# Dilated attention on one Trainium2 core: normalising each block's probabilities before their transpose, in place of scaling the finished outputs

## The chip, the core and the metric

The kernel runs on one core of one Trainium2 chip. The metric is the device time of one execution in microseconds (us); less is better. The engines named below are PE (TensorE: matrix products and transposes, writing to the PSUM banks), DVE (VectorE), ACT (ScalarE), POOL (GpSimd) and SP (which issues the DMAs). All of them run side by side and wait for each other through semaphores; each runs its own instructions in the order in which they were compiled.

## The reference, cut to what matters

One decoder layer with 1024 tokens and 1024 channels. Behind a joint input projection stand two mixers: a gated delta rule (4 heads of 128) and the dilated attention that this change touches (8 heads of 64). Its three branches share one softmax in effect, because their numerators and denominators are brought to a common maximum and added before the one division:

```python
    m_all = jnp.maximum(jnp.maximum(ms[0], ms[1]), ms[2])
    wts = [jnp.exp(mi - m_all) for mi in ms]
    num_tot = wts[0][..., None] * nums[0] + wts[1][..., None] * nums[1] + wts[2][..., None] * nums[2]
    den_tot = wts[0] * dens[0] + wts[1] * dens[1] + wts[2] * dens[2]
    out = num_tot / den_tot[..., None]
```

The mixers' outputs go through one output projection with a residual, then RMSNorm, a gated MLP with a short convolution, and a last RMSNorm. A division of every output row of a head by the denominator of its query gives the same value as a division of every probability of that query before the product with the values; this is the freedom that the change uses.

## The kernel before, in words

The program is emitted by several Python generators ("streams") that a small planner, the class `Weave`, interleaves. The planner keeps a clock `pe` of modelled TensorE time and, for every tile, the modelled time at which it is ready. A product advances the clock by the cost given at its call. An operation of another engine is charged by `account` with a fixed part and a part per element (DVE 0.07 + 0.00105 per element, ACT 0.12 + 0.00085, and 0.28 until the result may be used). A stream that needs a tile yields the time until that tile is ready; meanwhile the planner runs the ready stream with the lowest level number. TensorE's order is thereby fixed when the program is emitted (each PE instruction carries an order token); the order on the other engines is set when the program is compiled.

During the attention the streams that matter are `attention` (level 5) and `dense` (level 9). `dense` computes the input projection column by column; a column is 16 "triplets" of three passes (hi x hi, lo x hi, hi x lo), that is 48 matmuls of 128x128 by 128x512; it fills the clock wherever `attention` yields. The order of its columns is fixed (`DENSE`): the attention's own q, k and v of head pairs 1, 2 and 3, then the four gate columns z. `out_proj` (level 8) starts only when `dense` has ended.

Attention handles one pair of heads at a time (`pi`, 0 to 3), in two halves of the sequence (`hh`), each with four blocks of 128 queries (`u`; block number `n` = 4*hh + u). So there are 4 x 8 = 32 blocks and 8 groups of four. For a block:

- `scores` makes, for each head `e` of the pair, one PSUM bank of scores: 128 or 256 columns of near keys, and 128 (`hh` 0) or 256 (`hh` 1) columns of strided keys. The width `wd` is 256 for block 0, 384 for blocks 1 to 3 and 512 for blocks 4 to 7. DVE adds the mask, writes `sm` and accumulates the negated maximum (the profile lists it as CUSTOM_DVE_ANT and a read of the accumulator into `mx`); ACT takes the exponential in place (`sm<-sm,mx`) and accumulates the denominators into the tile `den` (line 853).
- `turn` transposes the probabilities on PE (`ps<-ident,sm`), and copies the near part to `pt` on DVE and the strided part to `pb` on ACT.
- `values` multiplies `pt` by the values (`ps<-pt,vn`) into the group's bank `po`, where the outputs stand transposed (head dimension on the partitions, queries along the free axis).
- After the group's fourth block `merge_classes` adds the strided part (`ps<-pb,vc`), takes the reciprocals of the group's denominators on DVE (`rd`, 128x8) and spreads them over 64 columns each (`rb`, 128x512).
- `normalise` runs two blocks later, from the list `queue`: four PE transposes turn `rb` (`ps<-ident,rb`), ACT copies them back to `rb`, and DVE multiplies `po` by `rb` into `oT` in another order of columns. SP stores `oT` in the scratch `mixer`, except that of the last group, which stays in SBUF.

The blocks are pipelined by `advance`: `scores(n)`, then `values(n-2)` (and the merge if that block was the fourth of its group), then `turn(n-1)`, then any `normalise` that is due. After the last block `advance(None)` runs four times to drain this.

Of the kernel before, what the change touches and what calls it, by code (L numbers as in the profile page):

```python
# [10 lines left out]
OP = mybir.AluOpType  # L11
# [123 lines left out]
def hybrid_layer(tc, I, out):  # L135
# [14 lines left out]
    def tile_(pool, shape, dt, name, tag, bufs):  # L150
        return wv.slot(pool.tile(list(shape), dt, name=name, tag=tag, bufs=bufs), tag, bufs)
# [75 lines left out]
    def next_bank(tag, *tiles, slack=0.0):  # L227

        while max(wv.need(*tiles), wv.slot_free(tag, 2)) + slack > 1e-3:
            yield max(wv.need(*tiles), wv.slot_free(tag, 2)) + slack  # L230
        return bank(tag)
# [581 lines left out]
    def attention():  # L813
        for h in range(H):
            yield from wv.until(("o", h))
        mks = [A("mk", "go") for _ in range(2)]
        sy.dma_start(mks[0], I["mk"][0])
        sy.dma_start(mks[1], I["mk"][1])
        yield from wv.until(("a", 0, 2))
        qkv = att_load(0)  # L820
        cur = qkv[:2] + (yield from att_values(qkv[2]))
        queue = []

        def mask(n):

            i, o, step, w, m = {0: (0, 128, 352, 128, 2), 1: (1, 0, 128, 128, 3), 2: (1, 384, 128, 128, 3),
                                3: (0, 608, 128, 128, 3)}.get(n, (0, 0, 480 - 32 * n, 256, 2))
            t = mks[i]
            return bass.AP(tensor=t.tensor, offset=t.offset + o, ap=[t.ap[0], [step, m], [1, w]]), m

        def scores(it):
            n, q, k, nb = it["n"], it["q"], it["k"], it["nb"]
            pss = [bank("asc") for _ in range(2)]
            yield wv.need(*pss, q, k)
            k0 = max(n - 1, 0) * P
            n1_, n2_ = (n + 1) * P - k0, P * nb
            wd = n1_ + n2_
            for e, er in enumerate(HALVES):
                mm(pss[e][:, :n1_], q[er, n * P:(n + 1) * P], k[er, k0:k0 + n1_], 0.0009 * n1_)
            for c in range(4):  # L840
                o = slice(32 * c, 32 * c + 32)
                for e, er in enumerate(HALVES):
                    mm(pss[e][o, n1_:wd].rearrange("p (n u) -> p n u", u=32), q[er, n * P + 32 * c:n * P + 32 * c + 32],
                       by_block(k)[er, :4 * nb, c, :], 0.00025 * n2_, tile_position=(64 * e, 32 * c))
            sm = A("sm", "dv*", shape=(P, 2, 512))
            mn = tile_(sp, [P, 2], F32, "mx", "mx", 4)
            mv, m = mask(n)
            for e in range(2):
                ve.tensor_tensor_reduce(out=sm[:, e, :wd].rearrange("p (a b) -> p a b", a=m),
                                        in0=pss[e][:, :wd].rearrange("p (a b) -> p a b", a=m), in1=mv, scale=-0.125,  # L850
                                        scalar=-NEG, op0=OP.add, op1=OP.min, accum_out=mn[:, e:e + 1])
            for e in range(2):
                ac.activation(sm[:, e, :wd], sm[:, e, :wd], AF.Exp, bias=mn[:, e:e + 1], scale=-1.0,
                              accum_out=it["den"][:, n, e:e + 1])
            it.update(sm=sm, wd=wd, n1=n1_, k0=k0)

        def turn(it):
            sm, wd, n1_ = it["sm"], it["wd"], it["n1"]
            it["pt"] = []
            for e in range(2):  # L860
                pt = tile_(sp, [P, 256], F32, "pt", "t1", 3)
                it["pt"].append(pt)
                pp = bank("atr")
                yield wv.need(pp, sm)
                for i in range(wd // P):
                    tp(pp[:, i * P:(i + 1) * P], sm[:, e, i * P:(i + 1) * P])
                ve.tensor_copy(pt[:, :n1_], pp[:, :n1_])
                ac.activation(it["pb"][e][:, it["u"]].rearrange("p b t -> p (b t)"), pp[:, n1_:wd], AF.Copy)

        def values(it):  # L870
            u = it["u"]
            yield wv.need(it["po"], *it["pt"])
            for i in range(it["n1"] // P):
                for e, er in enumerate(HALVES):
                    mm(it["po"][er, u * P:(u + 1) * P], v8(it["vn"])[:, it["k0"] // P + i, er],
                       it["pt"][e][:, i * P:(i + 1) * P], 0.12, u == 0 and i == 0, False, skip_group_check=True)

        def merge_classes(g):
            vcv = g["vc"].rearrange("p (c b d) -> p c b d", c=4, b=2)
            po, nb = g["po"], g["nb"]  # L880
            yield wv.need(*g["pb"])
            for c in range(4):
                for b in range(nb):
                    for e in range(2):
                        er = slice(64 * e, 64 * e + 64)
                        mm(po[er].rearrange("p (u t) -> p u t", u=4)[:, :, 32 * c:32 * c + 32],
                           vcv[:, c, b, er], g["pb"][e][:, :, b, 32 * c:32 * c + 32], 0.14,
                           False, c == 3 and b == nb - 1, skip_group_check=True)
            hh = g["hh"]
            rd = tile_(sp, [P, 4, 2], F32, "rd", "rd", 2)  # L890
            ve.reciprocal(rd, g["den"][:, 4 * hh:4 * hh + 4, :])
            rb = tile_(sp, [P, 512], F32, "rb", "t2", 2)
            ve.tensor_copy(rb.rearrange("p (a d) -> p a d", a=8),
                                  rd.rearrange("p u e -> p (u e)")[:, :, None].to_broadcast([P, 8, 64]))
            g["rb"] = rb

        def normalise(g):
            po, rb, hh = g["po"], g["rb"], g["hh"]
            oT = tile_(sp, [P, 512], F32, "oT", "t2", 2)
            pr = yield from next_bank("atr", rb, slack=ASLACK)  # L900
            for u in range(4):
                tp(pr[:, u * P:(u + 1) * P], rb[:, u * P:(u + 1) * P])
            ac.activation(rb, pr, AF.Copy)
            ve.tensor_tensor(
                oT.rearrange("p (n u c) -> p n c u", n=4, c=4),
                po.rearrange("p (n c u) -> p n c u", n=4, c=4),
                rb.rearrange("p (n c u) -> p n c u", n=4, c=4), op=OP.mult)
            if g["pi"] < 3 or hh == 0:
                sy.dma_start(mixer[4 + g["pi"]][:, half(hh)], oT)
            else:  # L910
                last["oT"] = oT
            if hh == 1:
                wv.done.add(("o", 4 + g["pi"]))


        pipe = []

        def advance(it):
            if it is not None:
                yield from scores(it)  # L920
            pipe.insert(0, it)
            if len(pipe) > 2:
                done = pipe.pop()
                if done is not None:
                    yield from values(done)
                    if done["u"] == 3:
                        yield from merge_classes(done["g"])
                        queue.append([1, done["g"]])
            if len(pipe) > 1 and pipe[1] is not None:
                yield from turn(pipe[1])  # L930
            for q in list(queue):
                q[0] -= 1
                if q[0] < 0:
                    yield from normalise(q[1])
                    queue.remove(q)

        for pi in range(4):
            q, k, vn, vc = cur
            den = sp.tile([P, NCH, 2], F32, name="den", tag="den", bufs=2)
            for hh in range(2):  # L940
                nb = 1 + hh
                if hh == 1 and pi < 3:
                    yield from wv.until(("a", pi + 1, 2))
                    qkv = att_load(pi + 1)
                po = bank("ch")
                pb = [A("pb", "qa", shape=(P, 4, nb, P)) for _ in range(2)]
                if pi == 3 and hh == 1:
                    wv.done.add("last group")
                g = dict(po=po, pb=pb, nb=nb, hh=hh, pi=pi, den=den, vc=vc)
                for u in range(4):  # L950
                    yield from advance(dict(n=4 * hh + u, u=u, q=q, k=k, vn=vn, nb=nb, po=po, pb=pb, den=den, g=g))
            if pi < 3:
                cur = qkv[:2] + (yield from att_values(qkv[2]))
        for _ in range(4):
            yield from advance(None)


# [517 lines left out]
```

## Time and profile before

| what | value |
|---|---|
| median of 3 runs | 1268.12 us (1267.27 to 1270.15) |
| the profiled execution, its own time | 1267.09 us |
| span of its trace, first to last instruction | 1263.9 us |
| mean granted TensorE clock | 0.992 |
| attention, first to last `sm` operation | 319 to 490 us, last `oT` at 498.3 us |
| `dense` ends, `out_proj` starts on PE | 521.7 us |
| PE, DVE, ACT, POOL busy over the span | 98%, 74%, 46%, 4% |

The profile page is one execution. Its first part gives the busy time of each engine. A line of the grouped view reads: source line, engine, operation, output tile <- input tiles, shapes, count | busy us, mean ns of one | idle time of the engine just before them and what ended it. Nearly all helpers record at line 131 (DVE and ACT), 176 (products) or 180 (transposes), so groups are told apart by their tiles. `PEld` is the weight load that precedes each product and overlaps the one before. Matmuls are pipelined: a 128x512 product is listed with 389 ns, while in an undisturbed stretch the next one starts 0.2275 us after it.

### The profile page before, as it was taken

The numbers are of one execution on the slowest core, as the hardware profiler recorded it, in microseconds if no ns is written. First come the engines' busy times: TensorE is split into PE (matmuls) and PEld (weight loads), VectorE is DVE, ScalarE is ACT, GpSimd is POOL, SyncE is SP. The second block draws the span as 40 slices with busy tenths as digits, with TensorE's granted clock in tenths as the row PEclk, the third lists the DMA queues.
The fourth block names the chain that finished last, engine by engine and source line by source line (L and its number), as shares of the span: only waits on it lengthen the run. The fifth ranks groups of instructions, "written<-read, shape, count | busy, mean of one in ns | idle before, by whom it ended". The sixth has DMA issues, their size and how long they took to land.

```text
span 1263.9 us, 18352 instructions
## 1 busy us (share of the span) xinstructions
PE 1240.5 (98%) x7102; PEld 1010.7 (80%) x7102; DVE 940.6 (74%) x1450; ACT 587.5 (46%) x1122; POOL 45.3 (4%) x34
## 2 busy tenths in 40 slices
PE   9999999999999999999999999999999999999996
PEld 7878887888677767878888888888888888787886
DVE  7575984573554455576888988988988979899875
ACT  7355534363544253365554444445445444343541
POOL 0012010022000000000000000000000000000000
PEclk9899999999999999999999999999999999999998
DMA  7022243345322411444323123123122198455623
GB/s 232 28 59 76 101 121 98 134 151 201 103 81 93 141 53 41 126 150 150 117 67 100 60 90 100 56 95 101 53 98 100 50 339 311 149 158 191 199 85 134
DMA packets 77766, 151.41 MB, mean 120 GB/s; under 512 B 21744, under 2 KB 28528, under 8 KB 77680
## 3 DMA queue, kind: packets, MB, share of 16 engines
q1 hardware_dynamic: 77680, 150.25, 36.1%
q8 instruction: 55, 0.90, 0.3%
q14 instruction: 31, 0.25, 0.1%
HBM read 112.21 MB, written 35.91 MB: 117 GB/s over the span
## 4 chain that ended last, share of the span: by engine, by line
PE 81%; DVE 8%; DMA 5%; issue 3%; ACT 2%; SPq 0%; POOL 0%; POOLq 0%; DVEq 0%; ACTq 0%
PE ps L176 42%; PE pa L176 18%; PE pc L176 9%; PE dw L176 8%; PE ps L180 4%; DMA wd<-in_wd 2%; DVE pr L131 2%; DMA r<-upark 1%; DVE x1h L131 1%; DVE kT L131 1%; DVE wd L131 1%; DVE r L131 0%; DMA wst<-in_wu 0%; DVE xr L131 0%; DMA xt<-in_xT 0%
## 5 line engine op out<-in xcount | busy, mean ns | idle before, releaser
L176 PE MATMUL dw<-pr 128*128 128x512 f32 (+1 forms) x984 | 213.4, 377 | 2.8 <-DVE x1h L131 2.0
L176 PEld LDWEIGHTS dw<-pr 128*128 128x128 f32 x984 | 176.1, 188 | 39.1 <-DVE x1h L131 4.2
L176 PE MATMUL ps<-xhi,whi 128*128 128x512 f32 x448 | 187.5, 419 | 2.0 <-DVE xr L131 2.0
L176 PE MATMUL ps<-xhi,wlo 128*128 128x512 f32 x448 | 177.0, 395 | 0.2 <-DVE wlo L131 0.2
L176 PE MATMUL ps<-xlo,whi 128*128 128x512 f32 x448 | 176.4, 394 | 0.0
L176 PE MATMUL pa<-T,pair 128*128 128x512 f32 x528 | 128.6, 393 | 0.7 <-ACT u L131 0.7
L176 PEld LDWEIGHTS pa<-T,pair 128*128 128x128 f32 x528 | 99.8, 189 | 21.8 <-ACT u L131 1.0
L176 PEld LDWEIGHTS ps<-xhi,whi 128*128 128x128 f32 x448 | 85.5, 191 | 19.4 <-issue 3.1
L176 PEld LDWEIGHTS ps<-xhi,wlo 128*128 128x128 f32 x448 | 85.0, 190 | 19.4 <-DVE wlo L131 0.6
L176 PEld LDWEIGHTS ps<-xlo,whi 128*128 128x128 f32 x448 | 85.7, 191 | 13.9
L131 ACT ACTIVATE u<-pa 128x512 f32<-128x512 f32 x44 | 26.3, 599 | 110.6 <-PE pa L176 110.6
L131 DVE SCALAR_TENSOR_TENSOR y<-xu,fcw,y 128x1023 f32<-128x1023 f32 (+1 forms) x44 | 56.4, 1281 | 25.7 <-ACT y L131 25.6
L131 ACT ACTIVATE whi<-wst 128x1024 fp32r<-128x1024 f32 (+2 forms) x38 | 38.6, 1016 | 68.8 <-PE ps L176 58.3
L176 PE MATMUL pa<-B,A 128*128 128x512 f32 x264 | 63.4, 389 | 0.0
L176 PE MATMUL pc<-T,S 128*128 128x512 f32 x264 | 63.4, 389 | 0.0
L176 PE MATMUL pa<-T,S 128*128 128x512 f32 x264 | 63.4, 389 | 0.0
L176 PE MATMUL pc<-B,pair 128*128 128x512 f32 x264 | 63.4, 389 | 0.0
L131 ACT ACTIVATE sm<-sm,mx 128x512 f32<-128x512 f32 (+2 forms) x64 | 41.5, 649 | 42.4 <-DVE mx L131 42.4
L131 DVE TENSOR_TENSOR wst<-wst 128x512 f32<-128x512 f32 x88 | 60.4, 686 | 0.8
L176 PE MATMUL ps<-B,pair 128*128 128x512 f32 x252 | 60.5, 389 | 0.0
L176 PEld LDWEIGHTS pc<-B,pair 128*128 128x128 f32 x264 | 49.6, 188 | 10.3
L176 PEld LDWEIGHTS pa<-B,A 128*128 128x128 f32 x264 | 49.6, 188 | 10.3
(233 smaller groups left out, 2280.4 us busy)
## 6 DMA issues: line engine op xcount, KB each, us to landing
wst<-in_wu SPq DMA_DIRECT2D x44, 512.0 KB, 3.6
wd<-in_wd SPq DMA_DIRECT2D x44, 512.0 KB, 4.0
wst<-in_wi SPq DMA_DIRECT2D x25, 512.0 KB, 3.7
upark<-y SPq DMA_DIRECT2D x22, 512.0 KB, 3.5
apark<-aqkv SPq DMA_DIRECT2D x12, 512.0 KB, 2.9
r<-upark SPq DMA_DIRECT2D x11, 512.0 KB, 7.9
r<-upark SPq DMA_DIRECT2D x22, 256.0 KB, 7.0
wa<-in_wd SPq DMA_DIRECT2D x22, 256.0 KB, 2.7
```

The source lines that it names most:

```text
L131: return getattr(eng, op)(*a, **kw)
L176: tc.stamp_issue_order_token(nc.tensor.matmul(dst, lhs, rhs, start=start, stop=stop, **kw).ins, TOKEN)
L180: tc.stamp_issue_order_token(nc.tensor.transpose(dst, src, ident).ins, TOKEN)
```

## The change

The denominators of a block no longer go to the tile `den` of the head pair but into two more columns of the block's own `mx` tile. DVE takes their reciprocals (128x2) as soon as both exponentials are done, and ACT multiplies each head's probabilities by them in place, with the reciprocal as a scale per partition. The transposes in `turn` then read the scaled probabilities. `merge_classes` no longer makes `rd` and `rb`; `normalise` and the list `queue` are gone. In their place `give`, called at once after the merge and without a wait in the planner, copies `po` to `oT` on DVE in the same changed order of columns and issues the same store. The drain after the last block is two steps instead of four.

```diff
             sm = A("sm", "dv*", shape=(P, 2, 512))
-            mn = tile_(sp, [P, 2], F32, "mx", "mx", 4)
+            mx = tile_(sp, [P, 4], F32, "mx", "mx", 4)
+            mn, den = mx[:, :2], mx[:, 2:]
...
                 ac.activation(sm[:, e, :wd], sm[:, e, :wd], AF.Exp, bias=mn[:, e:e + 1], scale=-1.0,
-                              accum_out=it["den"][:, n, e:e + 1])
+                              accum_out=den[:, e:e + 1])
+
+            ve.reciprocal(den, den)
+            for e in range(2):
+                ac.activation(sm[:, e, :wd], sm[:, e, :wd], AF.Copy, scale=den[:, e:e + 1])
...
-            hh = g["hh"]
-            rd = tile_(sp, [P, 4, 2], F32, "rd", "rd", 2)
-            ve.reciprocal(rd, g["den"][:, 4 * hh:4 * hh + 4, :])
-            rb = tile_(sp, [P, 512], F32, "rb", "t2", 2)
-            ve.tensor_copy(rb.rearrange("p (a d) -> p a d", a=8),
-                                  rd.rearrange("p u e -> p (u e)")[:, :, None].to_broadcast([P, 8, 64]))
-            g["rb"] = rb
-
-        def normalise(g):
-            po, rb, hh = g["po"], g["rb"], g["hh"]
+
+        def give(g):
+            po, hh = g["po"], g["hh"]
             oT = tile_(sp, [P, 512], F32, "oT", "t2", 2)
-            pr = yield from next_bank("atr", rb, slack=ASLACK)
-            for u in range(4):
-                tp(pr[:, u * P:(u + 1) * P], rb[:, u * P:(u + 1) * P])
-            ac.activation(rb, pr, AF.Copy)
-            ve.tensor_tensor(
-                oT.rearrange("p (n u c) -> p n c u", n=4, c=4),
-                po.rearrange("p (n c u) -> p n c u", n=4, c=4),
-                rb.rearrange("p (n c u) -> p n c u", n=4, c=4), op=OP.mult)
+            ve.tensor_copy(oT.rearrange("p (n u c) -> p n c u", n=4, c=4),
+                           po.rearrange("p (n c u) -> p n c u", n=4, c=4))
...
                     if done["u"] == 3:
                         yield from merge_classes(done["g"])
-                        queue.append([1, done["g"]])
+                        give(done["g"])
             if len(pipe) > 1 and pipe[1] is not None:
                 yield from turn(pipe[1])
-            for q in list(queue):
-                q[0] -= 1
-                if q[0] < 0:
-                    yield from normalise(q[1])
-                    queue.remove(q)
...
-        for _ in range(4):
+        for _ in range(2):
             yield from advance(None)
```

## The prediction

> **What bounds the kernel now.** I read the page's busy times first, then the chain of work that ended last, then the attention's stretch (319 to 499 us) as windows, groups by form, waits and timeline. From the page:
>
> ```profile
> PE 1240.5 (98%) x7102; PEld 1010.7 (80%) x7102; DVE 940.6 (74%) x1450; ACT 587.5 (46%) x1122; POOL 45.3 (4%) x34
> ...
> PE 81%; DVE 8%; DMA 5%; issue 3%; ACT 2%; SPq 0%; POOL 0%; POOLq 0%; DVEq 0%; ACTq 0%
> ```
>
> PE is busy nearly throughout and carries 81% of the chain. The windows (length, then busy us and count of PE, PEld, DVE, ACT, POOL) show that this holds in the attention, with room on the two engines that get the new work:
>
> ```profile
> 340.00:360.00 20.00, 20.00 (x227) 14.45 (x217) 10.32 (x31) 9.60 (x28) 0.00 (x0) 1.00 0.13 34
> ...
> 440.00:460.00 20.00, 20.00 (x226) 14.87 (x224) 10.77 (x32) 11.23 (x31) 0.00 (x0) 1.00 0.28 96
> 460.00:480.00 20.00, 18.87 (x213) 12.20 (x211) 13.53 (x34) 10.62 (x29) 0.00 (x0) 1.00 0.19 54
> ```
>
> ACT is busy at most 11.2 of 20 us. Only in one window, 460 to 480, does PE lose 1.1 us. The chain in order of time there (start, us, what), over one normalisation:
>
> ```profile
> 444.03 1.02 PE ps L180 x8
> 445.05 2.08 PE ps L176 x9
> 447.13 0.44 PE ps L180 x4
> 447.56 1.81 PE ps L176 x28
> ```
>
> That is a block's eight transposes, nine dense matmuls as filler, the four transposes of `rb`, then scores and values of the next block. All on PE, with no gap: whatever attention waits for, dense products cover it. Groups by form in 319 to 499, and the waits of PE's matmuls there:
>
> ```profile
> L180 PE MATMUL ps<-ident,rb 128*128 128x128 f32 x32 | 4.8, 272 | 0.0
> L176 PE MATMUL ps<-xhi,whi 128*128 128x512 f32 x115 | 48.2, 419 | 0.0
> L131 ACT ACTIVATE sm<-sm,mx 128x512 f32<-128x512 f32 x32 | 22.9, 716 | 25.3 <-DVE mx L131 25.3
> L131 ACT ACTIVATE pb<-ps 128x256 f32<-128x256 f32 x32 | 11.1, 374 | 5.0 <-DVE pt L131 4.5
> L131 DVE RECIPROCAL rd<-den 128x8 f32<-128x8 f32 x8 | 1.6, 203 | 2.3 <-ACT sm L131 2.3
> ...
> PE ps L176 <- DVE mx L131: 0.9, 1, 0.9
> PE ps L176 <- DVE pt L131: 0.2, 1, 0.2
> ```
>
> PE waited 1.1 us in all. So time here is PE's work, and a longer softmax costs something only where the filler is absent.
>
> **Removed from PE.** 32 transposes of `rb`, in eight pieces of four. The chain gives a piece 0.43 to 0.45 us: 8 x 0.44 = 3.5. I take -3.5. The 272 ns that the group lists for one is a pipelined duration; 32 x 0.272 = 8.7 is the far end. The Trainium skill, "TensorE: Matmul & The Clock Gate", section on the PE-mode transpose, gives about 275 ns for one in a kernel's context; by it the sum would be -8.8. The trace agrees with 275 as a duration, but four of them move the chain by 0.44, so as a cost the measurement decides against it.
>
> **Added to ACT, on the softmax path.** 64 scalings in place. The same form (128x512, SBUF to SBUF, copy with a scale per partition) is in the trace as `hb<-x,n`:
>
> ```profile
> L131 ACT ACTIVATE hb<-x,n x16: 707/712/727, 544.0 to 612.1; 128x512 f32<-128x512 f32 x16
> ```
>
> So 32 x 0.712 = 22.8; for 384 and 256 columns the exponentials bound it (608 and 502 ns): 24 x 0.608 + 8 x 0.502 = 18.6. With the eight `rb` copies gone (4.8), ACT gains 36.6 us over some 180. A wide block then needs, on ACT, two exponentials (0.72 apart), two scalings (1.42) and two `pb` copies (2 x 0.37): 3.6 us, 4.1 if it also idles 0.5 for the reciprocal in between. PE's work per wide block is 1.81 + 1.02 = 2.83 plus filler, below.
>
> **Added to DVE.** 32 reciprocals of 128x2: at most 0.203 (the 128x8 one), at least 0.085 (the accumulator read, 128x1), so 2.7 to 6.5 us. Gone are `rd` 1.6 and `rb` 3.4. The eight `oT` products (1.10 each) become copies: between 0.67 (the plain 128x512 PSUM read `xr`) and 1.10 (the permuted `aqkv`). Together -5.7 to +1.5, all beside PE work. Each reciprocal is a new wait for ACT at the head of DVE's queue. Queued behind it are the `pt` copies of the block before, dense's evacuations and the next block's masked maximum; PE waits for these last. The eight `rd` waited 0.3 us each; 32 such are 10 us of a DVE that is busy 10 to 13.5 of 20. The `mixer` stores stay seven; SP only sees them two blocks sooner, behind the same kind of wait.
>
> **Does the cover hold?** PE's order is set by the planner's arithmetic. For 512 columns, from the end of scores: 0.25, two maxima of 0.608, two exponentials of 0.555, each plus 0.28 because they share `sm`: ready at 3.70. The new steps add 0.072 and twice 0.555, plus 3 x 0.28: 5.72. On the chip a block whose scores ended at 479.67 had its exponentials done at 482.14, 2.47 later; add a hop of 0.17 (as from those scores to their maximum, begun at 479.83), 0.20 for the reciprocal, another hop and 1.43: 4.44. The planner leaves 1.3 us too much, so the order holds enough filler. How much does it take? `turn(n-1)` comes after `scores(n)` (0.97) and `values(n-2)` (0.48) and takes 0.88; without a merge two periods must cover 5.72 + 0.88 + 0.97, so one is 3.8 with some 2.5 triplets in it, before `turn` rather than before the transposes of `rb`. On PE that is 2.83 + 2.5 x 0.69 (2.08 for nine) = 4.6 us, above ACT's 4.1. The three blocks of a group without a merge take 22 matmuls, with nine for the value transposes some 53 per head pair; before, the pieces between 387 and 411 us hold 36 in a similar stretch, partly because each normalisation pulled in nine. Twelve blocks stand after the last forced stretch (411 to 435): 80 matmuls of the 192 in the z columns. Before, dense went on for 23 us after the attention (499 to 521.7), some 100 matmuls. So filler doesn't run out, and attention's end stays off the path: the first split of `oT` was at 536.8, 38 us after its making. Without that cover each block without a merge would cost up to 1.97 us (4.44 - 2.47).
>
> **Edges and stalls.** A dense matmul that follows other work costs about 0.1 more: xhi,whi averages 419 against 390 for the other two passes, 115 x 0.029 = 3.3 us over some 34 stretches. I count 32 to 40 stretches after: -0.2 to +0.6, taken as +0.2. The 1.1 us stall at 472 to 476, where a dense column ended and DVE had a weight split ahead of the maximum, may go (-1.1) or occur twice (+1.1): 0.
>
> **Sum.** -3.5 + 0.2 = -3.3 on the profiled 1267.09 (span 1263.9 and 3.2 around it): 1263.8. That run stands 1.0 below the median of three, so 1264.8 against 1268.12. By the bounds -3.5 - 0.2 - 1.1 to -3.5 + 0.6 + 1.1: 1263.3 to 1266.3. Behind 521.7 nothing changes but the start.
>
> **Rivals.** (1) *The gain is eaten by new stalls.* At the end of each dense column the planner has no filler for about a microsecond, and DVE then has 3 to 5 us of column work (two `aqkv` of 1.1 and a split of 1.2, or the z column's four steps). Some seven columns end inside the attention; one stalled before, two or three more at 1.1 to 1.9 give back 2 to 5: 1266 to 1270, say 1267.5. For it: the stall at 472. Against it: the longer spacing gives the maximum more room.
>
> (2) *ACT becomes the bound and it gets slower.* Place: the 24 blocks without a merge. It decides from the point where ACT needs more than 4.6 per wide block: at 4.1 plus a share of the split (1.05 per column, 0.2 per block) it needs 4.3. If each reciprocal waits a full microsecond more behind DVE's other work, ACT needs 5.3: 12 wide blocks x 0.7 = 8, half of that for the 12 narrow ones, less 3.3, is 9 more: 1277. For it: ACT would be at 90%. Against it: dense's DVE work touches one block in six.
>
> (3) *PE isn't the bound, and the softmax chain is.* PEld is busy only 14 to 15 of 20 us in the attention. Then the transposes are worth nothing and 32 blocks grow by up to 1.97 (4.44 - 2.47): +63, 1331; half hidden by the two-block pipeline, 1300. The Trainium skill, "Perfetto Trace Analysis", section Identifying the Most-Contended Engine, says this: matmul busy time is no good measure, LDWEIGHTS busy is. Against it here: a dense 128x512 matmul follows the last after 0.2275 us though its weight load takes only 0.19, so PEld at 80% is what a full PE shows.
>
> (4) *The transposes cost their listed time*: -8.7, 1259.6.
>
> **How the numbers follow.** A measurement here can tell 0.2%, 2.5 us (1265.6 to 1270.7), from no change. Chances: the forecast 0.52, (4) 0.04, (1) 0.28, (2) 0.13, (3) 0.03. Faster 0.56, same 0.28, slower 0.16. The range 1261.5 to 1271.5 leaves out (4), (3) and most of (2), and holds the rest.
>
> **What would show it.** Right: no `ps<-ident,rb`; PE's matmul records down by 32; dense matmuls ahead of the `sm` transposes; ACT in the attention's windows near 15 of 20; PE at 20.00 in them; `out_proj` starting near 518. Wrong: PE waiting for ACT `sm` or DVE `mx` in the windows, or dense ending before the last group's merge.

## The result, and the profile after

The changed kernel takes 1264.87 us (median of 20 runs, 1259.45 to 1267.07) against 1267.99 (20 runs, 1264.51 to 1270.95). The ratio is 0.9974, with a 95% interval of 0.9965 to 0.9984: faster by 3.1 us, a little more than the 0.2% that can be told from nothing.

The profiled execution of the changed kernel is one of its longer ones (1266.99 us), so spans alone would mislead. The place of the gain is read from two rows in each trace: the first product of the attention's scores, and the first product of `out_proj`, which follows the last dense product. The answers for the tiles `qT` and `ohi`, kernel before (count, ns min/median/max, first and last start):

```profile
L176 PE MATMUL ps<-kT,qT x640: 269/376/480, 318.3 to 484.7; 64*32 64x128 f32 x64, 64*32 64x256 f32 x64, 64*128 64x256 f32 x28, 64*128 64x128 f32 x4
L176 PE MATMUL ps<-ohi,whi x128: 387/389/504, 521.9 to 610.1; 128*128 128x512 f32 x128
```

and the changed kernel:

```profile
L176 PE MATMUL ps<-kT,qT x640: 269/376/481, 321.6 to 488.3; 64*32 64x128 f32 x64, 64*32 64x256 f32 x64, 64*128 64x256 f32 x28, 64*128 64x128 f32 x4
L176 PE MATMUL ps<-ohi,whi x128: 389/389/504, 522.3 to 610.4; 128*128 128x512 f32 x128
```

I call the time between the two "the stage". Both kernels do the same products in it (the same 444 dense matmuls by count), apart from the 32 turned reciprocals. It fell from 203.6 to 200.7 us. What stands ahead of it, untouched by the change, came 3.3 us late in this execution (in its first 60 us the granted clock averaged 0.91, against 0.94 before, which is about half of it), and what follows took 742.8 against 742.0. In a second trace of the changed kernel (run "changed again" below) the stage begins at 318.8 and takes 200.5 us, and 742.3 follow. So I put the gain of the 20 runs, 3.1 us, down to the stage's 2.9.

The page after, its lines on the engines and the chain:

```profile
PE 1241.6 (98%) x7070; PEld 1009.2 (80%) x7070; DVE 940.8 (74%) x1466; ACT 619.1 (49%) x1178; POOL 45.0 (4%) x34
...
PE 84%; DVE 6%; DMA 4%; issue 2%; ACT 2%; SPq 1%; POOLq 0%; POOL 0%; DVEq 0%; ACTq 0%
```

PE has 32 records fewer; ACT is busy 32 us longer. By the chain line PE's share grew from 81 to 84%, mostly at the cost of DVE (8 to 6%). The windows of the attention after (columns as before):

```profile
320.00:340.00 20.00, 19.86 (x181) 12.63 (x180) 9.75 (x32) 14.33 (x37) 0.00 (x0) 1.00 0.44 143
340.00:360.00 20.00, 19.77 (x200) 13.94 (x198) 12.33 (x33) 14.86 (x36) 0.00 (x0) 1.00 0.10 39
...
440.00:460.00 20.00, 20.00 (x199) 14.24 (x199) 10.64 (x34) 14.82 (x36) 0.00 (x0) 1.00 0.37 135
460.00:480.00 20.00, 20.00 (x203) 13.58 (x202) 13.49 (x36) 15.11 (x40) 0.00 (x0) 1.00 0.24 67
```

In these windows ACT is busy 14 to 15 of 20 us, where it was 9.6 to 11.2. PE stays all but full (it loses 0.14 and 0.23 us in the first two), and the window 460 to 480, where it had lost 1.1 us, is full. The chain there shows what went. Before, over the stretch of the stall (start us, us, what):

```profile
470.55 0.20 DVE rd L131
...
471.23 0.42 DVE rb L131
...
471.66 0.04 DVE wlo L131
471.70 1.10 issue
472.81 0.68 DVE sm L131
...
473.50 0.60 DVE sm L131
```

and after:

```profile
466.08 2.27 PE ps L176 x27
468.35 0.81 PE ps L180 x6
469.16 3.89 PE ps L176 x37
473.04 0.66 PE ps L180 x6
```

Before, DVE worked through `rd`, a gate column's `xr`, `rb` and a weight split before it came to the masked maximum that PE's next scores were waiting for. (The 1.10 us listed as "issue" pass while DVE does that split, `wlo`, which takes 1.23 us.) After, the chain in that stretch doesn't leave PE.

A tally of the stage, worked out from the trace: for every PE record the time from its start to the next record's start, summed by tile.

| PE time in the stage, us | before | changed | difference |
|---|---|---|---|
| transposes of `rb` (with the step to what follows) | 4.05 | 0 | -4.05 |
| scores | 35.93 | 34.97 | -0.96 |
| transposes of `sm` | 25.59 | 25.51 | -0.08 |
| dense products | 106.20 | 108.05 | +1.85 |
| values, merge, value transposes | 31.85 | 32.10 | +0.25 |
| sum | 203.62 | 200.64 | -2.98 |

Before, the stall stands in two of these rows: 1.0 us in the scores, and 1.0 at the end of one group of `sm` transposes, ahead of the scores that waited. So the row of the `sm` transposes, which comes out even, holds 0.9 us of new gaps elsewhere.

### The profile page after: what moved, and what is told of

It is laid out like the page before. It is cut to its first block, busy times and chain, and to the rows that moved or that the text cites. A ratio compares the mean times of both kernels' runs of the same rounds, so it can differ in the third digit from the quotient of the medians.

```text
span 1265.1 us, 18365 instructions
## 1 busy us (share of the span) xinstructions
PE 1241.6 (98%) x7070; PEld 1009.2 (80%) x7070; DVE 940.8 (74%) x1466; ACT 619.1 (49%) x1178; POOL 45.0 (4%) x34
## 4 chain that ended last, share of the span: by engine, by line
PE 84%; DVE 6%; DMA 4%; issue 2%; ACT 2%; SPq 1%; POOLq 0%; POOL 0%; DVEq 0%; ACTq 0%
PE ps L176 42%; PE pa L176 19%; PE dw L176 11%; PE pc L176 9%; PE ps L180 4%; DMA wd<-in_wd 1%; DVE pr L131 1%; DVE kT L131 1%; DVE x1h L131 1%; DMA xt<-in_xT 1%; DMA wst<-in_w 1%; SPq L131 1%; DVE wd L131 1%; DMA wst<-in_wu 0%; DVE xr L131 0%
## 5 line engine op out<-in xcount | busy, mean ns | idle before, releaser
L131 ACT ACTIVATE sm<-sm,mx 128x512 f32<-128x512 f32 (+2 forms) x128 | 79.6, 648 | 23.5 <-DVE mx L131 23.5
L131 ACT ACTIVATE pr<-wd 128x1024 fp32r<-128x1024 f32 x33 | 34.9, 1058 | 50.3 <-DVE wd L131 27.8
```

The source lines that it names most:

```text
L131: return getattr(eng, op)(*a, **kw)
```

## The experiments

Two theories stood against each other at first. Mine: PE alone sets the time of the stage, so the gain is the transposes' PE time, and the longer softmax costs nothing because dense products fill the wait. The rival: ACT or DVE sets it somewhere, and either the gain comes from their relief or the scalings eat part of a larger one. All ratios are to runs of the kernel before on the same chip, with 95% intervals; the stage is read as above, from one trace of each run.

| run | time, us | ratio (interval) | stage, us |
|---|---|---|---|
| before | 1267.99 | 1 | 203.6 |
| changed | 1264.87 | 0.9974 (0.9965 to 0.9984) | 200.7 |
| changed again | 1263.03 | 0.9958 (0.9943 to 0.9973) | 200.5 |
| changed, 32 transposes put back | 1267.03 | 0.9993 (0.9979 to 1.0008) | 203.5 |
| before, scalings added | 1267.78 | 1.0012 (0.9997 to 1.0026) | 204.9 |
| neither normalisation | 1263.03 | 0.9964 (0.9951 to 0.9977) | 198.0 |
| before, transposes of `rb` four times | 1281.10 | 1.0115 (1.0093 to 1.0136) | 214.0 |
| changed, scalings not charged | 1267.82 | 0.9991 (0.9978 to 1.0004) | 203.9 |
| changed, scaled twice | 1268.22 | 0.9999 (0.9983 to 1.0015) | 205.0 |
| changed, scaled three times | 1284.89 | 1.0129 (1.0111 to 1.0147) | 219.8 |
| changed, scaled on DVE | 1267.48 | 0.9993 (0.9978 to 1.0007) | 204.9 |
| changed, scalings charged more | 1262.94 | 0.9964 (0.9946 to 0.9982) | 200.1 |
| changed, one head on DVE, one on ACT | 1262.22 | 0.9954 (0.9941 to 0.9968) | 198.7 |

The changed kernel's stage repeats within 0.2 us (200.7 and 200.5), although its total moved by 1.8. The kernel before and the one with four times the transposes agree too: without the transposes of `rb` their stages are 199.6 and 199.5 us. This is why differences of 1 to 3 us are read from the stage; the other stages were not repeated.

### The transposes put back

```diff
         def give(g):
             po, hh = g["po"], g["hh"]
+            pr = yield from next_bank("atr")
+            for u in range(4):
+                tp(pr[:, u * P:(u + 1) * P], g["vc"][:, u * P:(u + 1) * P])
...
-                        give(done["g"])
+                        yield from give(done["g"])
```

> The changed kernel with four transposes put back per group, of a tile that nobody waits for (32 in all, their results are not used); softmax, scaling and DVE stay as changed. Theory (the gain is PE's work alone, 32 x 0.11 = 3.5 us): the gain goes, about 1268.2, ratio to before 1.000 (0.999 to 1.001). Rival (the gain comes from DVE and ACT, which lost rb, rd and the oT product, or from the shorter drain): stays at about 1265, ratio 0.9975.

Measured: 1267.03 us, ratio 0.9993, stage 203.5. The gain is gone from the stage to within 0.1 us, with softmax, ACT and DVE as in the changed kernel; the rival's 0.9975 lies just outside the interval. So PE's transposes are worth 2.8 to 3.0 us here, edges included: in the tally they take 3.9 us, and the transposes of `sm` get 1.3 back. That the stage ends so near to the one before is partly chance, since this run still pays for the scalings and doesn't have the old stall.

### The scalings alone

```diff
-                              accum_out=it["den"][:, n, e:e + 1])
+                              accum_out=own[:, e:e + 1])
+            ve.reciprocal(own, own)
+            for e in range(2):
+                ac.activation(sm[:, e, :wd], sm[:, e, :wd], AF.Copy, scale=own[:, e:e + 1])
...
+            ve.memset(den, 1.0)
```

> The kernel before with each block's reciprocals and 64 scalings added, the denominators of the later normalisation set to one, so that the turned reciprocals are still made and multiplied. It does alone what the change adds. Theory (ACT's 41 us and the longer softmax are covered by dense filler): as before, 1268 +- 1.3, ratio 0.999 to 1.001. Rival (the longer softmax costs PE waits that hide part of a larger gain): 1270 to 1275, ratio 1.002 to 1.006.

Measured: 1267.78 us, ratio 1.0012, stage 204.9, which is 1.3 us more. The ratio can't tell the theory's range from the rival's lower end. The stage says: nearly free, but not free.

### Neither

```diff
-            ve.reciprocal(den, den)
-            for e in range(2):
-                ac.activation(sm[:, e, :wd], sm[:, e, :wd], AF.Copy, scale=den[:, e:e + 1])
```

> The changed kernel without the reciprocals and scalings: the outputs of the attention are left unnormalised, so neither the turned reciprocals nor the scalings are paid. Theory (scaling is free): like the changed kernel, 1264.9 +- 1.3, ratio 0.9965 to 0.9985. Rival (scaling costs time): faster than the changed kernel by its cost, 2 us or more, ratio under 0.996.

This kernel leaves the attention's outputs undivided. Measured: 1263.03 us, ratio 0.9964, between the two: just below the theory's range and above the rival's 0.996, and the interval reaches into both. The stage is 198.0, 2.7 us below the changed kernel's. So the scalings do cost, and the change has given up about half of what dropping the old normalisation brings (5.6 us of stage). Total time alone would have hidden this: on another chip the changed kernel has the same median, 1263.03.

### What a transpose costs

```diff
-            for u in range(4):
-                tp(pr[:, u * P:(u + 1) * P], rb[:, u * P:(u + 1) * P])
+            for u in range(16):
+                tp(pr[:, (u % 4) * P:(u % 4 + 1) * P], rb[:, (u % 4) * P:(u % 4 + 1) * P])
```

> The kernel before with every transpose of rb made four times into the same bank, 96 more. It prices a transpose. Theory (0.11 us each, as the chain shows): +10.6 us, 1278.6, ratio 1.0083. Rival (each costs its listed 0.27 us): +26 us, 1294, ratio 1.0206. Rival (PE is not the bound there): no change, ratio 1.000.

The chain of this run, in order of time, at one normalisation:

```profile
451.96 2.08 PE ps L176 x9
454.04 1.75 PE ps L180 x16
455.78 1.81 PE ps L176 x28
```

Sixteen in 1.75 us where four took 0.44, and the stage grew by 10.4: 10.4 / 96 = 0.108 us each, although each is still listed with 270 to 273 ns. The total grew by more than the theory's 10.6: by the ratio 14.6 (11.8 to 17.2 by the interval, so 1.0083 lies outside). The profiled execution, 1276.59, is the shortest of the five and grew by 9.5; what the other 4 us are, no trace shows. The price from the stage stands, and 0.27 (26 us) and 0 are both excluded.

### Cover taken away

```diff
-            ve.reciprocal(den, den)
+            nc.vector.reciprocal(den, den)
             for e in range(2):
-                ac.activation(sm[:, e, :wd], sm[:, e, :wd], AF.Copy, scale=den[:, e:e + 1])
+                nc.scalar.activation(sm[:, e, :wd], sm[:, e, :wd], AF.Copy, scale=den[:, e:e + 1])
```

> The changed kernel with the reciprocals and scalings left out of the planner's account: it takes the probabilities to be ready 3.70 us after the scores, and places their transposes that early, while the chip needs some 4.4. It takes away cover and nothing else. Theory (filler is what makes the longer softmax free): PE now waits for ACT in front of the sm transposes; the 24 blocks without a merge lose 0.2 to 0.7 us each, 5 to 15 us, 1270 to 1280, ratio 1.002 to 1.009. Rival (PE is so far behind anyway that the planner's view of the softmax does not matter): as the changed kernel, ratio 0.996 to 0.9985.

Measured: 1267.82 us, ratio 0.9991, stage 203.9. The same instructions, only with PE's order made as if the scalings took no time: the whole gain is gone (3.2 us of stage). PE's order is, product for product, that of the run with neither normalisation. So in that order the scalings cost 5.9 us (203.9 against 198.0), and in the changed kernel's, with its added cover, 2.7. Cover is what makes them cheap, as expected, but the size was overrated: 0.9991 lies below the theory's range (its interval reaches only into the rival's), and not 24 blocks lost 0.2 to 0.7, but two lost 3.4 in all. Another 1.7 us went by a lower clock behind the first of these waits (last section). PE's waits between 319 and 540 us (us in total, times, longest; line 858 is the scaling there):

```profile
PE ps L180 <- ACT sm L858: 3.4, 2, 2.1
```

### ACT loaded until it decides

```diff
             for e in range(2):
                 ac.activation(sm[:, e, :wd], sm[:, e, :wd], AF.Copy, scale=den[:, e:e + 1])
+            for e in range(2):
+                ac.activation(sm[:, e, :wd], sm[:, e, :wd], AF.Copy, scale=ones[:, :1])
```

> The changed kernel with a second pass of 64 scalings (by one), charged in the planner: ACT then needs some 5.6 us for a wide block and the planner puts about four triplets ahead of the transposes, a PE period of 5.5. Theory (ACT costs nothing until its need passes PE's period): near the point where it decides, 1265 to 1269, ratio 0.9975 to 1.001. Rival (each scaling costs what the first pass seems to cost by the PE time of the stage, 200.6 us against 197.9 without it): 2.7 us more, 1267.6, ratio 0.9995, at least.

> As before with a third pass: ACT needs some 7 us for a wide block, PE's period by the planner is 6.3. Theory: now ACT decides in wide and narrow blocks, 0.5 to 0.9 us in each of 24, and the filler comes near its end: 1275 to 1290, ratio 1.006 to 1.018. Rival (still covered): 1265 to 1268.

The third pass repeats the added lines. Measured: 1268.22 us and stage 205.0 with two passes (4.3 more than the changed kernel by the stage), 1284.89 and 219.8 with three (14.8 more again). The second pass already costs more than the first (2.7, by the run with neither), the third more than three times the second. Up to 5 us of the 14.8 are a lower clock, at half for 6.8 and 3.4 us behind two waits of over 3 us. The window 340 to 360 of the run with two passes, and the same of the run with three:

```profile
340.00:360.00 20.00, 19.80 (x174) 13.96 (x173) 11.55 (x31) 18.71 (x42) 0.00 (x0) 1.00 0.17 54
```

```profile
340.00:360.00 20.00, 16.53 (x171) 10.59 (x171) 11.50 (x30) 18.72 (x43) 0.00 (x0) 1.00 0.20 68
```

With ACT at 18.7 of 20 us in both, PE loses 0.2 us in the first and 3.5 in the second. But this window is the mildest with two passes, where PE loses 4.3 us in all, as much as the stage grew. Another window of that run, and what PE's transposes waited for from 319 to 540 (0.7 us more is a wait of products for DVE):

```profile
440.00:460.00 20.00, 18.83 (x169) 13.58 (x168) 10.94 (x31) 17.80 (x40) 0.00 (x0) 1.00 0.41 146
```

```profile
PE ps L180 <- ACT sm L131: 3.6, 4, 1.2
```

The three longest waits, 1.1 to 1.2 us each, stand where no dense product lies ahead of the transposes of `sm`. So how full ACT is in a window doesn't tell what PE loses there. ACT as the bound is a real end of this road; it begins between the changed kernel's 14 to 15 of 20 us and the 16.3 to 18.7 that ACT has in the attention's busy windows with two passes. The rival's cost of at least 2.7 for the second pass fits too; only the third tells a growing cost from a constant one.

### The scalings on DVE, split, or charged more

```diff
-                ac.activation(sm[:, e, :wd], sm[:, e, :wd], AF.Copy, scale=den[:, e:e + 1])
+                ve.tensor_scalar(sm[:, e, :wd], sm[:, e, :wd], den[:, e:e + 1], None, op0=OP.mult)
```

> The changed kernel with the 64 scalings on DVE, as a multiplication by a scalar per partition, in place of ACT; the planner charges 0.608 in place of 0.555, so PE's order hardly changes. Theory (the small PE waits left in the changed kernel, 1.8 us by the gaps between PE's records, come from ACT being late): those waits go, 1262.5 to 1264.5, ratio 0.9955 to 0.997. Rival (DVE, with the masked maximum and the splits, is the one that comes late): 1266 to 1270, ratio 0.9985 to 1.0015.

Measured: 1267.48 us, stage 204.9: the theory fell, the rival's side holds. DVE's scaling is the shorter one (479 ns for 512 columns, where ACT's exponentials and scalings average 717), and still the stage grew by 4.2. PE's weight loads wait twice as long for DVE's masked maximum (`mx`). The changed kernel, waits between 319 and 530 us:

```profile
PEld ps L176 <- DVE mx L131: 4.9, 14, 0.4
PEld ps L176 <- DVE pt L131: 3.9, 10, 0.4
```

and with the scalings on DVE, 319 to 545 us:

```profile
PEld ps L176 <- DVE mx L131: 9.8, 27, 0.7
PEld ps L176 <- DVE pt L131: 4.3, 9, 0.7
```

By the planner's dearer DVE the dense products are also cut into 49 stretches in place of 41. Which of the two weighs more, this run doesn't say.

The next two ran beside the changed kernel on one chip. One charges each scaling more in the planner (`ac2 = Engine(wv, nc.scalar, "scalar", 0.3, 0.00105)`), the other splits them:

```diff
-            for e in range(2):
-                ac.activation(sm[:, e, :wd], sm[:, e, :wd], AF.Copy, scale=den[:, e:e + 1])
+            ve.tensor_scalar(sm[:, 0, :wd], sm[:, 0, :wd], den[:, :1], None, op0=OP.mult)
+            ac.activation(sm[:, 1, :wd], sm[:, 1, :wd], AF.Copy, scale=den[:, 1:])
```

> The changed kernel once more, beside the next two on the same chip. 1263.5 to 1266, ratio 0.996 to 0.9985; PE time from the first scores to the end of dense 200.6 us.

Measured: 1263.03 us, ratio 0.9958, both a little under the expected ranges; the stage, 200.5, is as expected.

> The changed kernel with each scaling charged 0.84 us in the planner for 512 columns, in place of 0.555, which is nearer to the 0.71 and the queue that the chip shows; the instructions are the same, PE's order has more filler ahead of the transposes. Theory (the 1.8 us of PE gaps before transposes and merges are ACT's lateness against the planner's clock): they go, the stage falls to 198.5 to 200 us, ratio 0.995 to 0.997. Rival (more cuts into dense cost as much at the edges, about 0.1 us each): stage 200.5 to 202, ratio as the changed kernel's.

> The changed kernel with the first head's scaling on DVE and the second's on ACT, side by side on the chip. Theory (either engine alone comes late at times: ACT with two scalings per block, DVE with two): with one each, the gaps fall below the changed kernel's, stage 198.5 to 200.5 us, ratio 0.995 to 0.998. Rival (what DVE's scalings cost is that the planner's order changes, 49 cuts into dense against 41): stage 202 to 205, ratio 0.998 to 1.001.

Charged more: 1262.94 us, stage 200.1, 0.4 below the changed kernel's. The waits of PE's matmuls for ACT are gone, and by the steps between PE's records some 1.5 us of gaps; the other order, with 43 stretches of dense products for 41, took 1.1 back. The stage lies between theory and rival, so this settles little. Split: 1262.22 us, inside what the theory expected; stage 198.7, 1.8 below the changed kernel's and 0.7 above the one that doesn't normalise at all. Its windows:

```profile
320.00:340.00 20.00, 20.00 (x195) 12.96 (x195) 13.74 (x42) 12.15 (x35) 0.00 (x0) 1.00 0.29 80
340.00:360.00 20.00, 20.00 (x219) 14.63 (x217) 13.92 (x39) 14.59 (x36) 0.00 (x0) 1.00 0.17 54
```

PE is full from 320 on, where the changed kernel had lost 0.14 and 0.23 in these two windows, with DVE and ACT both below 15. It beats the kernel before (0.9954, 0.9941 to 0.9968). Against the changed kernel only the stage speaks for it: the two ratios' intervals overlap.

## Why the prediction was right, step by step

The forecast was 1264.8 us, and 1264.87 was measured; the sum of -3.3 stands against -3.1 in the runs and -2.9 in the stage. That closeness is in part luck. Gaps and edges, put at 0 and +0.2, cost about 3 us; the end of a stall that was put at 0 paid for most of it. The signs named for it came, but for two: `out_proj` started at 522.3 and not near 518, 3.3 us of it from the late start of the stage, and PE was at 19.8 to 19.9 of 20 us in two windows.

- **The transposes, -3.5.** Right, and shown from both sides: put back, they cost 2.8 to 3.0; multiplied, 0.108 each, 3.5 for 32. The rival price of 0.27 fell. The Trainium skill's 275 ns ("TensorE: Matmul & The Clock Gate", Part 4: PE-mode transpose) agrees with the duration the traces list (270 to 273). As a cost it doesn't hold here: the next one starts 0.108 us later.
- **PE is the bound.** Right: of the third rival (PE not the bound, PEld at 14 of 20 us) nothing is left, since 96 more transposes lengthened the stage by their own time. The Trainium skill ("Perfetto Trace Analysis", Identifying the Most-Contended Engine) judges PE's headroom by how busy the weight loads are, beside the achieved share of peak; here they were busy some 70% of the time (14 of 20 us), and there was no headroom.
- **The softmax path is covered, 0.** The step that was mis-sized. It costs 2.7 us by the run without scalings, 1.3 when added to the kernel before. In the changed kernel's PE records I find some 1.8 us of small gaps ahead of and among the transposes of `sm` and at the merges, each under 0.45; the other 0.9 of the 2.7 are hand-overs between kinds of products (41 stretches of dense against 37). The length was judged well: a block whose scores ended at 481.12 had its scalings done at 485.73, 4.6 later, where 4.44 was worked out. But it was set against the blocks without a merge, where the filler stands; most of the gaps lie where the planner puts none: between the two heads' transposes and ahead of a merge, where PE waits for a `pb` copy that ACT does late.
- **Edges, +0.2.** Too small. Dense is cut into 41 stretches against 35 (32 to 40 were counted), and 24 of them end at scores or values, against 16. Each cut costs about 0.1 at its start, as put, and another 0.1 at such an end (0.33 us to the next start, where it is 0.23 when transposes follow), which wasn't in the sum: 6 x 0.1 + 8 x 0.1 = 1.4 of the +1.85 in the tally.
- **The stall at 472 to 476, 0.** It went, and it was worth more than the bound of -1.1: about 1.0 in scores and 1.0 ahead of them. That covers most of the two errors above. That DVE no longer holds `rb` and `rd` there is seen in the chain; that this is why it went, and not merely the changed order of PE, was not tried apart.
- **ACT and DVE.** The `sm` activations grew by 38.1 us (41.4 put), the reciprocals took 5.1 (2.7 to 6.5) and waited 11.0 for ACT (10). The `oT` copy takes 1.095, as long as the product had: the upper bound.

Of the rivals, the first (new stalls eat the gain) happened in part, and an old stall's end paid for it. The second (ACT decides) needs one more pass of scalings.

## What to carry to other kernels

Work moved from a full engine to idle ones is worth what it took from the full one only so long as the order on the full engine makes room for the longer path; the same instructions with the order made for a shorter path lost the whole gain. Price an instruction on a pipelined engine by how far it moves the next one's start, not by its listed duration, and count a cut into a long stretch of products at both ends. Where two half-idle engines can each take half of a step, try that before giving it to the one that is faster at it; here only the stage of one trace speaks for it.

## What the runs showed of the hardware

A PE wait costs more than itself when it is long enough. With the scalings not charged, PE waited for ACT ahead of one block (its matmuls idled 2.13 us, its weight load 2.56, until 331.61), and then the granted clock fell. Windows of that run:

```profile
328.00:331.00 3.00, 1.48 (x7) 0.83 (x7) 2.26 (x7) 2.09 (x9) 0.00 (x0) 1.00 0.19 38
331.00:335.00 4.00, 3.39 (x12) 2.84 (x12) 1.02 (x3) 2.56 (x7) 0.00 (x0) 0.57 0.54 164
335.00:339.00 4.00, 4.00 (x48) 2.43 (x47) 1.86 (x7) 1.73 (x6) 0.00 (x0) 1.00 0.41 131
```

The clock column (the third from the right) goes 1.00, 0.57, 1.00; by the trace it is at half for 3.4 us from 331.2. Dense matmuls listed with 0.39 to 0.40 us took 0.63 there. With three passes of scaling a wait of 3.2 us, until 404.5, was followed by seven microseconds at 0.51, and one of 3.1 us, until 512.1, by another 3.4 us at half. Waits of 1.4 and 1.5 us in the same run left the clock at 1.00, and so did all of those with two passes, none longer than 1.4. Between the two lies a length at which it may go either way: some 70 us from the start every trace has a PE wait of 1.97 us, and in ten of the 13 traces the clock was at half for 3.4 us within about 1 us of its end, in three it stayed at 1.00. The Trainium skill ("TensorE: Matmul & The Clock Gate", Why this matters for your kernels) warns of idle gaps of PE over about 3 us between bursts of matmuls; here 2.0 to 2.1 us was often enough.
